# A hybrid attention encoder layer on one core: the first four loads on three queues, five spinning matmuls in place of six, and other queues for the last two stores

## The chip, the cores and the metric

The kernel runs on one core of one Trainium2 chip. The metric is device time of one execution in microseconds (us). Each kernel is run several times, and the median counts. One execution is also profiled: its span, and every instruction in it, is what the profile shows.

## The reference

One layer over x, 1024 tokens of 1024 channels in float32. A single projection `h = x @ W_in` gives queries, keys, values and gates of two groups of heads. Group A attends in a 2-D neighbourhood of the token grid with a learned bias, group B in a window of 128 with rotary positions and a sink. Each output is multiplied by SiLU of its gate, all are projected by `W_out`, and the layer ends in a layer norm:

```python
h = jnp.einsum('bsd,de->bse', x, w_in[layer])
q_a, k_a, v_a, z_a, q_b, k_b, v_b, z_b = jnp.split(h, SPLIT_POINTS, axis=-1)
...
mixed = jnp.concatenate([y_a * jax.nn.silu(z_a), y_b * jax.nn.silu(z_b)], axis=-1)
y = jnp.einsum('bse,ed->bsd', mixed, w_out[layer])
x = layer_norm(DEEPNORM_ALPHA * x + y, ln_gain[layer], ln_bias[layer])
```

## The kernel before

All matmuls of weights are made of three products: each operand is split into a high and a low part, and high by high, low by high and high by low are added up in PSUM.

**The head.** The first stage computes the values v of both groups, 640 columns, for tokens in tiles of 128. It walks over the eight slices k of 128 channels. For each k it needs one tile of x (`xT[half, k]`, 128 channels by 512 tokens) and one of the weights (`wv[k]`, 128 by 640). `load_x` and `load_wv` are generators that yield after every instruction, so that `interleave` can emit a load, a cast to the high part and a subtraction for the low part of both in turn. The rounding of wv to its high part runs on ScalarE (L414), that of x on VectorE for the first tile and on ScalarE for the others (L398), and the low parts on VectorE (L401, L417).

Only for k=0 are the tiles loaded in two pieces: `load_wv(0, (0, 320, 640))` and `load_x(0, 0, (0, 256, 512))`. Three calls of `next` ahead of the interleaving put the order of the four issues on the queue of SyncE (SP in the profile): left wv, left x, right x, and then right wv. The raw tiles come from pools of three buffers (wv) and four (x), so the loads for k=1 and k=2 go out at once behind these, and from k=3 on SyncE waits for a buffer.

The matmuls `v_mms` (L430) have x as their stationary operand and wv as the moving one, 320 columns at a time, in eight banks: four token tiles `t` by two halves `a` of wv. For k=0 the passes are the outer loop: first high by high over all eight banks, the left half of wv for the four token tiles and then the right half, then the two other passes. So the first two matmuls need the left wv and the left x, the third and fourth the right x, and the fifth to eighth the right wv. From k=1 on the three passes of one bank stand together, so that the second matmul of k=1 needs the low part of the second x tile.

Ahead of these, a memset of `warm` and six matmuls on it (L390) keep TensorE busy; nothing reads their result. GpSimd (POOL) builds the identity `identf` at the same time, which a transpose reads much later (L453). ScalarE's first instruction is the load of its activation table.

From the value stage on the order of instructions is written out by hand (`manual_schedule`); the part ahead of it is ordered by a scheduler.

**The tail.** After the last output matmuls of the eighth token tile, `norm_last` normalises its 1024 columns in three parts: `h0`, columns 0 to 255, and `h1`, 256 to 863, on VectorE (L968, L971 and then L975 for `h1` and `h0` in this order), and `h2`, the last 160, on ScalarE and GpSimd (L970, L972, L973). The stores of `h1` and `h0` are issued by SyncE (L976), that of `h2` by ScalarE (L977).

Of the kernel before, what the change touches and what calls it, by code (L numbers as in the profile page):

```python
# [55 lines left out]
def hybrid_block(ctx, tc, xT, x, wt, wv, wo, bias, sink, gain, lbias, cos, sin, bmask, out):  # L56
    nc = tc.nc
# [10 lines left out]
    def bank(tag):  # L68
        bufs = {"pj": 2, "s": 4, "t": 2}[tag]
        return (ps1 if bufs == 1 else ps2).tile([128, 512], F32, tag=tag, name=f"ps_{tag}", bufs=bufs)  # L70
# [311 lines left out]
    with ExitStack() as vctx:  # L382
# [3 lines left out]
        warm = vp.tile([128, 512], F16, name="warm", bufs=1)  # L386
        nc.vector.memset(warm, 0.0)
        ps = bank("t")
        for _ in range(6):
            nc.tensor.matmul(ps, warm[:, :128], warm, start=True, stop=True)  # L390

        def load_x(half, k, cuts=(0, 512)):
            raw = vp.tile([128, 512], F32, tag="xr", name="xraw", bufs=4)
            for a, b in zip(cuts, cuts[1:]):
                nc.sync.dma_start(raw[:, a:b], xT[half, k, :, a:b])
                yield
            for a, b in zip(cuts, cuts[1:]):
                (nc.scalar.copy if len(cuts) == 2 else nc.vector.tensor_copy)(xh[half, k][:, a:b], raw[:, a:b])  # L398
                yield
            for a, b in zip(cuts, cuts[1:]):  # L400
                nc.vector.tensor_sub(xl[half, k][:, a:b], raw[:, a:b], xh[half, k][:, a:b].bitcast(F32))  # L401
                yield

        def load_wv(k, cuts=(0, 640)):
            raw = vp.tile([128, 640], F32, tag="wvr", name="wvraw", bufs=3)
            for a, b in zip(cuts, cuts[1:]):
                nc.sync.dma_start(raw[:, a:b], wv[k, :, a:b])
                yield
            h = vw.tile([128, 640], F32R, name=f"wvh{k}")
            l = vw.tile([128, 640], F32R, name=f"wvl{k}")  # L410
            wvh.append(h)
            wvl.append(l)
            for a, b in zip(cuts, cuts[1:]):
                nc.scalar.copy(h[:, a:b], raw[:, a:b])  # L414
                yield
            for a, b in zip(cuts, cuts[1:]):
                nc.vector.tensor_sub(l[:, a:b], raw[:, a:b], h[:, a:b].bitcast(F32))  # L417
                yield
# [75 lines left out]
        banks = [bank(t) for t in tags]  # L494
        ordered.enter_context(tc.manual_schedule())
        first = load_wv(0, (0, 320, 640)), load_x(0, 0, (0, 256, 512))
        for i in (0, 1, 1):
            next(first[i])
        interleave(*first)
        interleave(load_wv(1), load_x(0, 1))  # L500
        for k in range(KT):
            if k + 2 < KT:
                interleave(load_wv(k + 2), load_x(0, k + 2))
            if k >= X1AT:
                interleave(load_x(1, 2 * (k - X1AT)))
                interleave(load_x(1, 2 * (k - X1AT) + 1))
                x_max(0, k - X1AT)
            for ps in ([0], [1], [2]) if k == 0 else ([0, 1, 2],):
                for a in range(2):
                    for t in range(4):  # L510
                        v_mms(banks[2 * t + a], t, a, k, ps)
# [240 lines left out]
    def quad(q):  # L752
        g, p, j, t, _ = units[4 * q]
        return g, p, j, t // 4 if g == "b" else t[0] // 2
# [161 lines left out]
    def final():  # L916
# [32 lines left out]
        def row_stats(t):  # L949
            mv = fp.tile([128, 2], F32, tag="mv", name="mv")  # L950
            nc.vector.bn_aggr(mv, stats[t][:, :4 if t == 7 else 2, :])  # L951
            sd = fp.tile([128, 1], F32, tag="sd", name="sd")
            nc.scalar.activation(sd, mv[:, 1:2], AF.Sqrt, bias=eps)  # L953
            return mv, sd

        def row_scale(mv, sd):
            rstd = fp.tile([128, 1], F32, tag="rstd", name="rstd")
            nc.vector.reciprocal(rstd, sd)
            nmr = fp.tile([128, 1], F32, tag="nmr", name="nmr")
            nc.vector.scalar_tensor_tensor(nmr, mv[:, 0:1], -1.0, rstd, op0=ALU.mult, op1=ALU.mult)  # L960
            return rstd, nmr

        def norm_last(t):
            ts = slice(128 * t, 128 * t + 128)
            xr = xrs[t]
            mv, sd = row_stats(t)
            h0, h1, h2 = slice(0, 256), slice(256, 864), slice(864, 1024)
            nc.vector.scalar_tensor_tensor(xr[:, h0], xr[:, h0], mv[:, 0:1], gb[:, h0], op0=ALU.subtract, op1=ALU.mult)  # L968
            rstd, nmr = row_scale(mv, sd)
            nc.scalar.activation(xr[:, h2], xr[:, h2], AF.Identity, bias=nmr, scale=rstd)  # L970
            nc.vector.scalar_tensor_tensor(xr[:, h1], xr[:, h1], mv[:, 0:1], gb[:, h1], op0=ALU.subtract, op1=ALU.mult)  # L971
            nc.gpsimd.tensor_mul(xr[:, h2], xr[:, h2], gb[:, h2])  # L972
            nc.gpsimd.tensor_add(xr[:, h2], xr[:, h2], bb[:, h2])  # L973
            for h in (h1, h0):
                nc.vector.scalar_tensor_tensor(xr[:, h], xr[:, h], rstd, bb[:, h], op0=ALU.mult, op1=ALU.add)  # L975
                nc.sync.dma_start(out[ts, h], xr[:, h])  # L976
            nc.scalar.dma_start(out[ts, h2], xr[:, h2])  # L977

        def norm(t):
            ts = slice(128 * t, 128 * t + 128)  # L980
# [44 lines left out]
        with tc.manual_schedule():  # L1025
            norm_last(7)
# [11 lines left out]
    for i in range(-LD, NU + LO):  # L1038
# [5 lines left out]
        per, h = divmod(i, 16)  # L1044
# [23 lines left out]
        q, m = divmod(i - LP - 3, 4)  # L1068
        if i >= Q30 + 2:
            q, m = (NU // 4 - 2, i - Q30 - 2) if i < Q30 + 4 else divmod(i - LP - 3, 4)  # L1070
        elif i >= Q30:
            q, m = -1, 0
# [9 lines left out]
        if 0 <= q < NU // 4:  # L1082
            g, p, j, h = quad(q)
# [88 lines left out]
```

## Time and profile before

| | |
|---|---|
| median of three runs | 455.44 us (455.09 to 457.77) |
| the profiled execution | 455.45 us |
| its span | 453.7 us |
| TensorE busy with matmuls | 443.1 us, 98% of the span |
| VectorE, ScalarE, GpSimd busy | 333.9, 288.0 and 228.1 us |
| DMA, mean over the span | 181 GB/s |

Times in the profile count from the start of the span. PE is TensorE's matmul row and PEld its row of weight loads, DVE is VectorE, ACT ScalarE, POOL GpSimd and SP SyncE; a q behind a name is the sequencer of that engine, which issues DMAs. The page cuts the span into 40 slices of 11.3 us:

```profile
PE   8999999999999999999999999999999999999993
...
DMA  7897278984557796687889779999989877004511
```

Each digit is a busy share in tenths. TensorE is short of nine tenths only in the first slice and the last, and these hold the lines that are changed.

### The profile page before, as it was taken

The page shows a single profiled execution, that of the slowest core. Times are in us where ns is not written, and L with a number is a line of the kernel's source. Part 1 is how long each engine was busy: PE and PEld are TensorE (multiplying, and loading weights), DVE is VectorE, ACT ScalarE, POOL GpSimd, SP SyncE. Part 2 cuts the span into 40 slices and gives each one's busy share as a digit, 9 for nine tenths or more (in the row PEclk, how much of TensorE's full clock was granted, in tenths as well). Part 3 has the DMA queues.
Part 4 walks back from the last instruction along what each step waited for, and adds up shares of the span by engine and source line. Part 5 has one row for each costly group of instructions (what it writes and reads, how often), then busy time and mean ns, then how long its engine had stood idle before and what let it go on. Part 6 is the DMA issues. An engine that isn't in the chain of part 4 may idle for free.

```text
span 453.7 us, 9395 instructions
## 1 busy us (share of the span) xinstructions
PE 443.1 (98%) x3239; PEld 293.1 (65%) x3239; DVE 333.9 (74%) x808; ACT 288.0 (63%) x664; POOL 228.1 (50%) x235
## 2 busy tenths in 40 slices
PE   8999999999999999999999999999999999999993
PEld 6999974444445565555555656555556788888883
DVE  5885956538987777896888878877878739099644
ACT  5648649776489877788778887686878824012100
POOL 0003944546948559688326766446663444007621
PEclk9999999999999999999999999999999999999997
DMA  7897278984557796687889779999989877004511
GB/s 249 291 320 266 76 247 259 309 307 177 208 103 167 151 176 152 112 176 139 167 154 174 174 161 216 190 175 232 188 166 225 165 230 286 0 17 147 187 54 61
DMA packets 134415, 82.28 MB, mean 181 GB/s; under 512 B 101344, under 2 KB 113504, under 8 KB 134112
## 3 DMA queue, kind: packets, MB, share of 16 engines
q1 hardware_dynamic: 134224, 81.61, 72.3%
q8 instruction: 25, 0.41, 0.4%
q14 instruction: 22, 0.18, 0.2%
q10 hardware_dynamic: 144, 0.08, 0.1%
HBM read 51.25 MB, written 9.96 MB: 135 GB/s over the span
## 4 chain that ended last, share of the span: by engine, by line
PE 91%; DVE 3%; issue 2%; ACT 2%; DMA 1%; SPq 0%; DVEq 0%; ACTq 0%
PE ps_pj L356 44%; PE ps_s L899 9%; PE ps_t L774 6%; PE ps_s L430 6%; PE ps_pj L899 6%; PE ps_t L899 5%; PE ps_s L709 4%; PE ps_s L710 4%; PE ps_pj L430 3%; PE ps_t L430 3%; PE ps_t L794 1%; DVE qs L241 1%; DMA wvraw<-in_wv 1%; ACT split L745 1%; DVE split L746 1%
## 5 line engine op out<-in xcount | busy, mean ns | idle before, releaser
L356 PE MATMUL ps_pj<-xf,wh 128*128 128x512 f16 x672 | 202.1, 379 | 0.9 <-DVE qs L241 0.6
L356 PE MATMUL ps_pj<-xf,wl 128*128 128x512 f16 x336 | 127.3, 379 | 0.0
L356 PEld LDWEIGHTS <-wh 128*128 128x128 f16 x672 | 63.5, 98 | 61.6 <-DVE ks L241 1.1
L735 ACT ACTIVATE ps_s<-sn,nm 128x385 f32<-128x385 f32 (+3 forms) x128 | 70.3, 549 | 32.8 <-DVE nm L719 31.7
L746 DVE SCALAR_TENSOR_TENSOR split<-ps_s,split 128x384 f16<-128x384 f32 (+2 forms) x128 | 65.7, 513 | 27.7 <-ACT split L745 26.3
L745 ACT ACTIVATE split<-ps_s 128x384 f16<-128x384 f32 (+2 forms) x128 | 57.6, 450 | 1.8
L356 PEld LDWEIGHTS <-wl 128*128 128x128 f16 x336 | 32.9, 98 | 37.4
L719 DVE CUSTOM_DVE_ANT_0 sn<-ps_s,bm,nsk 128x384 f32<-128x384 f32 (+1 forms) x64 | 40.8, 638 | 6.8 <-PE ps_s L710 6.2
L899 PE MATMUL ps_s<-wo,m 128*128 128x512 f32 (+1 forms) x192 | 43.3, 379 | 0.0
L719 DVE CUSTOM_DVE_ANT_0 sn<-ps_s,bias,sg 128x264 f32<-128x264 f32 (+1 forms) x64 | 35.0, 548 | 10.9 <-PE ps_s L710 4.7
L187 POOL TENSOR_SCALAR wr<-wr,wsc 128x512 f32<-128x512 f32 x26 | 20.7, 796 | 39.8 <-ACT wh L182 33.7
L709 PE MATMUL ps_s<-ks,qs 128*128 128x384 f16 (+4 forms) x128 | 39.3, 307 | 0.0
L710 PE MATMUL ps_s<-ks,qs 128*128 128x384 f16 (+4 forms) x128 | 39.2, 306 | 0.0
L899 PEld LDWEIGHTS ps_s<-wo,m 128*128 128x128 f32 x192 | 34.4, 188 | 7.0
L774 PEld LDWEIGHTS <-tr 128*128 128x128 f16 (+1 forms) x1104 | 36.5, 98 | 2.2 <-issue 0.3
L681 POOL TENSOR_SCALAR bias<-bias,rsg 128x552 f32<-128x552 f32 (+1 forms) x24 | 19.3, 802 | 36.4 <-DMA bias<-in_bias 25.5
L953 ACT ACTIVATE sd<-mv,eps 128x1 f32<-128x1 f32 x8 | 2.4, 295 | 50.5 <-DVE mv L951 46.5
L188 POOL TENSOR_TENSOR wl<-wr,wh 128x512 f16<-128x512 f32 x26 | 32.6, 1256 | 2.2
L273 POOL COPY ks<-ks 64x512 f16<-64x512 f16 x40 | 26.4, 666 | 10.9 <-DVE ks L241 6.1
L989 POOL TENSOR_TENSOR xr<-xr,gb 128x512 f32<-128x512 f32 x7 | 10.3, 1474 | 40.8 <-ACT xr L986 40.8
L430 PE MATMUL ps_s<-wvh,x 128*128 128x320 f32 x128 | 29.5, 310 | 0.0
L899 PE MATMUL ps_pj<-wo,m 128*128 128x512 f32 (+1 forms) x120 | 28.7, 377 | 0.0
(147 smaller groups left out, 825.6 us busy)
## 6 DMA issues: line engine op xcount, KB each, us to landing
xraw<-in_xT SPq DMA_DIRECT2D x31, 256.0 KB, 4.3
ws<-in_wt SPq DMA_DIRECT2D x15, 512.0 KB, 5.2
wr<-in_wt SPq DMA_DIRECT2D x26, 256.0 KB, 3.0
bias<-in_bias SPq DMA_DIRECT2D x16, 276.0 KB, 3.4
wor<-in_wo SPq DMA_DIRECT2D x16, 256.0 KB, 3.2
xr<-in_x SPq DMA_DIRECT2D x8, 512.0 KB, 7.3
out<-xr SPq DMA_DIRECT2D x14, 256.0 KB, 2.1
bias<-in_bias SPq DMA_DIRECT2D x8, 368.0 KB, 3.9
```

Source lines behind the costliest of these rows:

```text
L188: nc.gpsimd.tensor_sub(l, raw, h)
L273: nc.gpsimd.tensor_copy(t[o, sl], t[a, sl])
L356: nc.tensor.matmul(ps, a[:, k % 4, :], mv, start=(k == 0 and i == 0), stop=(k == KT - 1 and i == 2))
L430: nc.tensor.matmul(ps[:, :320], lh[t // 4, k][:, ts], rh[k][:, cs], start=(k == 0 and i == 0), stop=(k == KT - 1 and i == 2))
L709: nc.tensor.matmul(ps[:, :m], q, sl[0], start=True, stop=False)
L710: nc.tensor.matmul(ps[:, :m], q, sl[1], start=False, stop=True)
L719: nc.vector.tensor_tensor_reduce(sn[:, :m], ps[:, :m], bias_t, sg[:, c:c + 1], init, op0=ALU.add, op1=ALU.min, accum_out=nm)
L735: nc.scalar.activation(pt[:, :m], sn[:, :m], AF.Exp, bias=nm, scale=-1.0, accum_out=sm[:, k:k + 1])
L745: nc.scalar.activation(hl[:, :m, 0, :c], src, AF.Copy, scale=PSCALE)
L746: nc.vector.scalar_tensor_tensor(hl[:, :m, 1, :c], src, PSCALE, hl[:, :m, 0, :c], op0=ALU.mult, op1=ALU.subtract)
L774: nc.tensor.matmul(ps[:, HD * m:HD * m + HD], a, b_, start=(i == 0), stop=(i == len(mms) - 1))
L899: nc.tensor.matmul(ps, lh[:, ts], rh[:, cs], start=(e == EO[0] and i == 0), stop=(e == EO[-1] and i == 2))
```

## The change

The four first loads are spread over three queues. `load_x` with three cuts (the first tile alone) issues its left piece from ScalarE and its right piece from SyncE; `load_wv` issues the left or only piece from SyncE and, where there is a second, that one from GpSimd. The spinning matmuls are five. In `norm_last` the store of `h0` goes to ScalarE and that of `h2` to SyncE, behind that of `h1`.

```diff
-        for _ in range(6):
+        for _ in range(5):
             nc.tensor.matmul(ps, warm[:, :128], warm, start=True, stop=True)
...
-            for a, b in zip(cuts, cuts[1:]):
-                nc.sync.dma_start(raw[:, a:b], xT[half, k, :, a:b])
+            for q, a, b in zip((nc.scalar, nc.sync) if len(cuts) == 3 else (nc.sync,), cuts, cuts[1:]):
+                q.dma_start(raw[:, a:b], xT[half, k, :, a:b])
                 yield
...
-            for a, b in zip(cuts, cuts[1:]):
-                nc.sync.dma_start(raw[:, a:b], wv[k, :, a:b])
+            for q, a, b in zip((nc.sync, nc.gpsimd), cuts, cuts[1:]):
+                q.dma_start(raw[:, a:b], wv[k, :, a:b])
                 yield
...
-            for h in (h1, h0):
+            for h, q in ((h1, nc.sync), (h0, nc.scalar)):
                 nc.vector.scalar_tensor_tensor(xr[:, h], xr[:, h], rstd, bb[:, h], op0=ALU.mult, op1=ALU.add)
-                nc.sync.dma_start(out[ts, h], xr[:, h])
-            nc.scalar.dma_start(out[ts, h2], xr[:, h2])
+                q.dma_start(out[ts, h], xr[:, h])
+            nc.sync.dma_start(out[ts, h2], xr[:, h2])
```

In the order of instructions on each engine nothing else moves. ScalarE's new load stands ahead of its table load. GpSimd's stands between the memset of `identf` and the instruction that makes the identity of it. On SyncE the order behind is left wv, right x, wv for k=1, x for k=1, and so on as before.

## The prediction

> **What bounds the kernel now.** I read the page first: TensorE (PE) is busy 443.1 us of a 453.7 us span, so only about 10.6 us are open at all. The table of waits, asked for TensorE alone, has four entries: 1.3 us until the spinning matmuls start, 0.7 us in the first projection step, and 0.6 and 0.4 us in the middle. The change touches the first ten microseconds and the last four. So the chain of waits of the first 14 us comes next (start, length, what):
>
> ```profile
> 0.74 0.39 SPq L407
> 1.19 0.42 SPq L395
> 1.65 0.43 SPq L395
> 2.12 3.02 DMA wvraw<-in_wv
> 5.17 0.47 ACT wvh L414
> 5.68 0.41 PE ps_pj L430
> ```
>
> SyncE issues the four first loads one after the other, some 0.46 us apart. The fourth, the right half of the first wv tile, takes 3.02 us to land, ScalarE rounds it, and TensorE then goes on. The timeline shows both sides of that wait and the next place where loads and TensorE meet (start, length, engine, line, operation, idle time before it):
>
> ```profile
> 1.33 2.74 PE L390 MATMUL ps_t<-warm 128*128 128x512 f16 x6 [1.33 <-DVE warm L387]
> 3.92 0.60 PE L430 MATMUL ps_pj<-wvh,x 128*128 128x320 f32 x1
> ...
> 4.70 0.30 PE L430 MATMUL ps_s<-wvh,x 128*128 128x320 f32 x1
> ...
> 5.68 0.41 PE L430 MATMUL ps_pj<-wvh,x 128*128 128x320 f32 x1 [0.67 <-ACT wvh L414]
> ...
> 7.40 0.62 ACT L398 CAST x<-xraw 128x512 fp32r<-128x512 f32 x1 [0.34 <-DMA xraw<-in_xT]
> ...
> 8.05 0.69 DVE L401 TENSOR_TENSOR x<-xraw,x 128x512 fp32r<-128x512 f32 x1
> ...
> 8.72 0.49 PE L430 MATMUL ps_pj<-wvh,x 128*128 128x320 f32 x2
> ```
>
> From 5.68 the matmuls start 0.147 us apart. The fourth started at 4.70, so the fifth could have started at 4.85: the wait is worth 5.68 - 4.85 = 0.83 us. But look at step k=1: its second matmul needs the low part of the second x tile, ready at 8.05 + 0.69 = 8.74, and TensorE is there at 8.72 + 0.15 = 8.87. The slack is 0.1 us. Whatever is gained in step k=0 waits again in k=1, unless that x tile lands earlier too. So the landing of the second x tile (7.40 now) is the row that prices the change. Step k=2 doesn't matter: its x cast ends at 9.50 and TensorE needs it near 12.1.
>
> Is that landing limited by issue or by the DMA engines? The windows of a quarter microsecond answer (window, length, busy time of each engine, clock, DMA share, GB/s):
>
> ```profile
> 4.00:4.25 0.25, 0.25 (x2) 0.25 (x2) 0.25 (x2) 0.00 (x0) 0.00 (x0) 1.00 1.21 297
> 4.75:5.00 0.25, 0.25 (x2) 0.00 (x0) 0.25 (x2) 0.00 (x0) 0.00 (x0) 1.00 0.70 261
> 5.00:5.25 0.25, 0.00 (x1) 0.00 (x0) 0.22 (x1) 0.08 (x1) 0.00 (x0) 1.00 0.59 205
> 5.25:5.50 0.25, 0.00 (x0) 0.00 (x0) 0.00 (x0) 0.25 (x1) 0.00 (x0) 1.00 0.58 219
> 6.00:6.25 0.25, 0.25 (x4) 0.25 (x3) 0.15 (x1) 0.00 (x0) 0.00 (x0) 1.00 1.00 383
> ```
>
> The sixteen engines are nearly full except between 4.75 and 5.50, a hole of 0.25 x (0.30 + 0.41 + 0.42) = 0.28 us, and in the ramp from 1.75 to 2.50 (shares 0.59, 0.82 and 0.92, so 0.17 us). The tail, timeline again:
>
> ```profile
> 448.83 1.72 DVE L975 SCALAR_TENSOR_TENSOR xr<-xr,rstd,bb 128x608 f32<-128x608 f32 x2
> 449.31 0.95 POOL L973 TENSOR_TENSOR xr<-xr,bb 128x160 f32<-128x160 f32 x1
> 449.91 0.99 SPq L976 DMA_DIRECT2D out<-xr  x2
> 450.29 0.37 ACTq L977 DMA_DIRECT2D out<-xr  x1
> ```
>
> SyncE's two issues take 0.33 each in 0.99 us, so the second starts at 450.57, just after VectorE's last result at 450.55: it waits for its data and not for the queue. The last two parts already leave on two queues.
>
> **The change part by part.** *Loads.* The left half of x goes from SyncE's second place (1.19) to ScalarE's first instruction (0.73). The one ScalarE DMA that the trace has was issued in 0.37 us, as fast as SyncE's. The activation table load (1.28 us from 0.73) moves behind it and ends near 2.45; ScalarE's first cast waits for data until 2.96, so 0.5 us of that cover is left and the cost is nothing. The right half of x moves on SyncE from 1.65 to 1.19. The right half of wv leaves SyncE (2.12) for GpSimd, behind one memset that ends at 0.93. The mask instruction for the identity behind it is delayed, and its first reader is the transpose at 38.1: nothing. Everything behind on SyncE (second wv tile, second x tile and so on) is issued two places earlier: 2 x 0.46 = 0.92 us.
>
> The first matmul (3.92) needs the left wv (landed 2.96, cast 0.46) and the left x (landed 3.48, cast 0.29). Both transfers now start together and share the engines. By the bytes both should be there when both were before, near 3.48: then the wv cast ends at 3.94 where x was ready at 3.77, so the start moves by 0.0 to 0.3 us later. The wait of 0.83 absorbs that: the fifth matmul waits for the right wv, issued up to 1.2 us earlier, and 576 KB in all must land, which before was at 5.17.
>
> So the gain is how much earlier the second x tile lands. Bounds: 0 if the engines' share alone counts; 0.92 if issue alone counts, of which TensorE can use the 0.83. Between them I take 0.3: the hole of 0.28 is what a slow load at the head of a single queue leaves, and it is the part that three queues can fill; of the ramp I count almost nothing.
>
> *Five spinning matmuls.* 2.74 us for six, their weight loads 0.43 apart: the sixth frees TensorE near 3.86, the fifth near 3.43. The first real weight load was at 3.89, with x ready at 3.77: at most 0.1 us, and none where data come at 3.9 or later. Zero.
>
> *Tail.* The last 256 columns go to ScalarE, the 160 columns to SyncE, free at 450.24 when its data are done at 450.26. Issue to landing is 2.1 us on SyncE and 2.2 on ScalarE in the table of DMA issues. Bounds -0.05 (an own queue) and +0.1; I take +0.05.
>
> Sum against the profiled execution: 455.45 (span 453.7 and 1.75 around it), which is also the median of the runs (455.44): 455.45 - 0.3 + 0.05 = 455.2. TensorE waits only 1.0 us after the head and before the tail, so the shift passes through.
>
> **The rivals.** *The transfers only interleave.* The windows speak for it: shares near 1 before and after the hole, and 1152 KB must land before k=1 can go on. Then the 0.83 moves from k=0 to the second matmul of k=1, the gain is 0, and with the tail the time is 455.5. The Trainium skill says this outright (DMA: Bandwidth & Descriptors, "Issuing engines are not separate DMA queues"): loads from several engines run on the same sixteen DMA engines, and only the issue time is saved. By that rule this rival holds; the trace agrees in the full windows and not in the hole.
>
> *GpSimd's load comes late: slower.* No load in this trace is issued by GpSimd. The place is the fifth matmul, and it decides from a landing at 5.1 on; from there a microsecond costs a microsecond. The nearest rows, 160 KB on SyncE, took 2.2 and 3.0 us: from 0.93 that is 3.1 to 3.9, well before. The longest of the head (the third x tile, 4.8) gives 5.7, a loss of 0.6 and 456.1; with another microsecond for a first use, 457.1. Against it stands 1.2 us of margin. The Trainium skill (SBUF — State Buffer, "SBUF: two separate sides") warns that descriptors written by GpSimd wait while VectorE holds the port they share. Here VectorE does two short memsets until 1.27 and then nothing until 3.48, so the trace gives it little to hold.
>
> *The clock comes later: slower too.* The spinning matmuls run 0.43 us per 512 columns, the real ones from 5.68 on 0.147 per 320: 0.83 against 0.46 ns a column, though the granted clock reads 1.00 throughout. The switch came near 4.5, after 3.2 us of work from 1.33. With five spins TensorE idles from 3.46 to about 3.9. If the count began anew at the first real matmul (3.9), TensorE would run slowly to 7.1, which is 12 of the 24 matmuls of k=0, and do the other 12 in 1.8 us, to 8.9 where it now ends near 8.72; begun anew behind the wait, near 5.0, it would run slowly to 8.2, 16 matmuls in all, and end at 9.4. A loss of 0.2 to 0.7: 455.9. Against it: the gap of 0.83 before 5.68 did not slow anything.
>
> *The whole wait is collected.* If the second x tile lands by 6.6, nothing waits and all of 0.83 is gained: 454.7.
>
> **How the numbers follow.** Forecast 455.2 (its own range 454.9 to 455.4): 0.45. Interleaving, 455.5: 0.20. GpSimd late, 456.1: 0.15. Clock late, 455.9: 0.10. All collected, 454.7: 0.10. The range 454.5 to 456.5 leaves out the far end of the two slow cases. About 1% (4.55 us) is what a measurement of this kernel can tell from no change; its three runs alone span 2.7 us. No case comes near 450.9 or 460.0. I leave 0.02 and 0.03 for what I don't see.
>
> **What would show it.** Right: the idle time before the fifth projection matmul shrinks from 0.67 to under 0.2, the cast of the second x tile starts near 7.1, step k=1 waits a little before its second matmul, and the tail from VectorE's last result to the end of the span is as long as before (3.1 us). Interleaving: that cast at 7.4 still. GpSimd late: ScalarE's second cast after 5.2, released by GpSimd's load. Clock: projection matmuls 0.27 us apart after 5 us. The forecast is wrong in its mechanism if the second x tile lands earlier by 0.3 and the span is not shorter, or if the time moves by over 1 us.

## The result and the profile after

The changed kernel takes 457.95 us (median of 22 runs), the kernel before on the same chip 455.99 us (22 runs). The ratio is 1.0031, with a 95% interval from 1.0016 to 1.0046: slower by 0.3%. The two medians are further apart (1.96 us), because that of the changed kernel falls into the upper of two groups of runs; the means of all runs are 1.41 us apart, as the ratio has it. Counts and ranges of runs below leave out one disturbed run of 574 us, of the kernel with eight spins.

The runs of the changed kernel fall into two groups. Eight lie between 455.93 and 456.78, fourteen between 457.50 and 459.46. Of the kernel before, four of 22 lie above 457. The profiled execution (span 457.0, 3.3 us longer than before) is one of the upper group.

The chain of waits of its first 14 us, with start, length and what:

```profile
1.30 4.97 DMA wvraw<-in_wv
...
6.29 0.47 ACT wvh L414
...
6.80 0.63 PE ps_pj L430
7.43 0.27 PE ps_s L430
...
11.17 0.27 PE ps_s L430
11.44 0.25 PE ps_pj L430
11.69 0.14 PE ps_s L430
```

The load of the right half of the first wv tile, now GpSimd's, is still the link that everything waits for. It took 3.02 us from issue to landing, and takes 4.97 now. Behind it the matmuls of step k=0 stand 0.27 us apart up to 11.5 us, where before they stood 0.15 apart from the fifth on. The timeline gives the same stretch instruction by instruction:

```profile
1.30 0.74 POOL L407 DMA_DIRECT2D wvraw<-in_wv  x1 [0.35 <-issue]
...
1.34 2.31 PE L390 MATMUL ps_t<-warm 128*128 128x512 f16 x5 [1.34 <-DVE warm L387]
...
3.44 0.46 ACT L414 CAST wvh<-wvraw 128x320 fp32r<-128x320 f32 x1 [0.97 <-DMA wvraw<-in_wv]
...
4.07 0.61 PE L430 MATMUL ps_pj<-wvh,x 128*128 128x320 f32 x1 [0.41 <-DVE x L398]
...
6.80 0.63 PE L430 MATMUL ps_pj<-wvh,x 128*128 128x320 f32 x1 [1.33 <-ACT wvh L414]
...
7.65 0.62 ACT L398 CAST x<-xraw 128x512 fp32r<-128x512 f32 x1
...
11.96 0.46 PE L430 MATMUL ps_pj<-wvh,x 128*128 128x320 f32 x2
```

The fifth real matmul starts at 6.80, 1.12 us later than before. Step k=1 starts at 11.96 where it started at 8.72: from the fifth matmul to there it takes 5.16 us, where it took 3.04. So 2.12 us more are the slow matmuls, 1.12 the wait: 3.24 in all. Idle time stands now ahead of the first real matmul too (0.41), where the sixth spin stood. And the second x tile, issued 0.94 us earlier, is cast from 7.65 on, not from 7.40: nothing was won there.

The four loads, from the table of DMA issues for the first 1.9 us (size, and us from issue to landing):

```profile
wvraw<-in_wv SPq DMA_DIRECT2D x1, 160.0 KB, 2.7
wvraw<-in_wv POOLq DMA_DIRECT2D x1, 160.0 KB, 5.0
xraw<-in_xT ACTq DMA_DIRECT2D x1, 128.0 KB, 2.9
xraw<-in_xT SPq DMA_DIRECT2D x1, 128.0 KB, 2.7
```

Before, these took 2.2, 3.0, 2.3 and 2.2. The prediction had seen a hole in the DMA share between 4.75 and 5.50 us (0.70, 0.59 and 0.58). Three quarter-microsecond windows of the changed kernel show where it went (the last two numbers are the DMA share and GB/s):

```profile
2.00:2.25 0.25, 0.25 (x2) 0.08 (x1) 0.00 (x0) 0.25 (x1) 0.15 (x2) 1.00 0.23 36
...
3.75:4.00 0.25, 0.00 (x0) 0.00 (x0) 0.24 (x2) 0.14 (x1) 0.00 (x0) 1.00 0.57 102
...
5.25:5.50 0.25, 0.22 (x1) 0.00 (x0) 0.04 (x1) 0.00 (x0) 0.00 (x0) 1.00 1.03 305
```

From 4.75 to 5.50 the shares are now 1.03, 0.69 and 1.03, but from 2.00 to 2.50 they are 0.23 and 0.57 and from 3.50 to 4.25 they are 0.55, 0.57 and 0.43. Over 1.50 to 5.50 the engines moved 212 GB/s, before 228. The hole was filled and others opened earlier. The tail, timeline:

```profile
451.88 1.71 DVE L975 SCALAR_TENSOR_TENSOR xr<-xr,rstd,bb 128x608 f32<-128x608 f32 x2
452.37 0.95 POOL L973 TENSOR_TENSOR xr<-xr,bb 128x160 f32<-128x160 f32 x1
452.96 0.33 SPq L976 DMA_DIRECT2D out<-xr  x1
453.39 0.38 SPq L977 DMA_DIRECT2D out<-xr  x1
453.63 0.36 ACTq L976 DMA_DIRECT2D out<-xr  x1
```

From VectorE's last result (453.59) to the end of the span are 3.39 us, before 3.11. Sum against the profile of before: 3.24 in the head, 0.28 in the tail and 0.2 less in the 437 us between them make the 3.3.

### The profile page after: what moved, and what is told of

Read it like the earlier page. It is cut to its first block, busy times and chain, and to the rows that moved or that the text cites. A ratio compares the mean times of both kernels' runs of the same rounds, so it can differ in the third digit from the quotient of the medians.

```text
span 457.0 us, 9394 instructions
## 1 busy us (share of the span) xinstructions
PE 445.1 (97%) x3238; PEld 295.3 (65%) x3238; DVE 333.6 (73%) x808; ACT 287.8 (63%) x664; POOL 228.4 (50%) x236
## 4 chain that ended last, share of the span: by engine, by line
PE 91%; DVE 3%; issue 2%; ACT 2%; DMA 1%; DVEq 0%; POOL 0%; POOLq 0%; ACTq 0%
PE ps_pj L356 44%; PE ps_s L899 9%; PE ps_t L774 6%; PE ps_s L430 6%; PE ps_pj L899 6%; PE ps_t L899 5%; PE ps_s L709 4%; PE ps_s L710 4%; PE ps_pj L430 3%; PE ps_t L430 3%; PE ps_t L794 1%; DMA wvraw<-in_wv 1%; DVE qs L241 1%; ACT split L745 1%; DVE split L746 1%
## 5 line engine op out<-in xcount | busy, mean ns | idle before, releaser
L430 PE MATMUL ps_s<-wvh,x 128*128 128x320 f32 x128 | 30.8, 320 | 0.0
```

The costliest lines, as they stand in the source:

```text
L430: nc.tensor.matmul(ps[:, :320], lh[t // 4, k][:, ts], rh[k][:, cs], start=(k == 0 and i == 0), stop=(k == KT - 1 and i == 2))
```

## The experiments

Twelve runs in four sets, each set beside the kernel before on the same chip. Theories A and B are about what makes the clock late: A the missing spin, B the long wait for the load. Theory C came after the first four.

**Five spins alone.** In the kernel before:

```diff
-        for _ in range(6):
+        for _ in range(5):
```

> The kernel before with five spinning matmuls; loads and stores as before. Theory A (the missing spin lets TensorE idle near 3.6 us, and the clock comes late): matmuls 0.27 us apart beyond 6 us in most runs, median about 457.3. Theory B (the long wait for GpSimd's load makes the clock late): the spin alone does nothing, median about 456.0 as before.

Measured: 456.23 against 455.64, ratio 1.0012 (1.0003 to 1.0022). In its profile the matmuls are 0.27 apart up to 6.8 us. One run of twelve lies above 457. The missing spin costs something, so B alone falls; it costs far less than the change, so A alone falls too.

**Six spins with the new loads and stores.** In the changed kernel:

```diff
-        for _ in range(5):
+        for _ in range(6):
```

> The changed kernel with six spinning matmuls. Theory A: the clock comes as early as before, and only the late load remains: median 456.5 to 457. Theory B: the fifth matmul still waits to 6.8 us and the clock is late: 458, as the changed kernel. Either way GpSimd's load lands near 6.3 us.

Measured: 456.46 against 455.64, ratio 1.0024 (1.0015 to 1.0033). In its profile the load lands at 5.6, a little better than expected, but matmuls stay slow to 10.0 us. That profile is of one of the two slowest runs (457.73); eight of the eleven runs lie between 456.18 and 456.61, and what the clock did in them is not shown. So the sixth spin does not bring the clock back in every run. The median is A's, the late clock of the profile B's.

**No GpSimd.** In the changed kernel the right wv is issued by ScalarE:

```diff
-            for q, a, b in zip((nc.sync, nc.gpsimd), cuts, cuts[1:]):
+            for q, a, b in zip((nc.sync, nc.scalar), cuts, cuts[1:]):
```

> The changed kernel with the right half of the first wv tile issued by ScalarE behind the left x, not by GpSimd; five spins. If the load was late because GpSimd issued it: it lands near 4.7 us, the fifth matmul starts near 5.3, and step k=1 waits for the second x tile near 7.4. If it was late because three queues share the engines: near 6 us again. Theory A: the clock is still late in most runs, median about 457; theory B: 455.7.

Measured: 456.79 against 455.64, ratio 1.0024 (1.0014 to 1.0034). The timeline of its profile:

```profile
4.07 0.90 ACT L414 CAST wvh<-wvraw 128x320 fp32r<-128x320 f32 x2 [1.15 <-DMA wvraw<-in_wv]
...
4.58 0.64 PE L430 MATMUL ps_pj<-wvh,x 128*128 128x320 f32 x1 [0.94 <-ACT wvh L414]
```

The right wv is there at 4.5, as expected without GpSimd, but the left one, which the first matmul needs, lands 1.1 us later than before (cast at 4.07, not 2.96). The idle time moved from the fifth matmul to the first. The clock rises at 9.3.

**Spins in the wait.** In the changed kernel, ahead of the fifth real matmul:

```diff
+                    if k == 0 and ps == [0] and a == 1:
+                        for _ in range(3):
+                            nc.tensor.matmul(banks[1], warm[:, :128], warm, start=True, stop=True)
                     for t in range(4):
```

> The changed kernel with three more spinning matmuls between the fourth and the fifth real one, into a bank that the fifth overwrites. The load stays late. If idle time of TensorE delays the clock, it comes before 8.2 us and the median is 456.5 to 457; if the clock has nothing to do with the idle time, 458 as the changed kernel.

Measured: 457.15 against 455.64, ratio 1.0030 (1.0017 to 1.0043), half of eight runs above 457. The profile, of a run in the faster half (456.38), did what was expected: the clock is up by 6.8, step k=1 starts at 9.59, the span is 454.6. The median did not, and from one profile it can't be said where the other runs lost their time. A miss.

These four profiles and those of the two kernels led to theory C. Until some moment, which is called here the rise of the clock, TensorE's matmuls of 320 columns start 0.27 us apart, and 0.15 us from there on. The Trainium skill (TensorE: Matmul & The Clock Gate, "Part 1: The HAM clock gate (the "warmup" mystery)") says that the clock is decided over windows of about 3.4 us that run on freely and don't start with the kernel. It does not say how much idle time such a window may hold. The table is an estimate, worked out from the starts of the matmuls with that page's figure for the window. Idle is all time beyond 0.43 us for a spinning matmul and 0.27 us for a slow real one, so it includes the slower start of a matmul behind a wait:

```
kernel               clock rises near   idle in the 3.4 us ahead   idle in the 3.4 us before those
before               4.6                0.4                        -
e1 five spins        6.8                0.7                        1.3
e4 spins in wait     6.1 to 6.8         0.8 to 0.9                 1.4 to 2.0
e2 loads, six spins  10.0               0.0                        1.35
e3 two queues        9.3                0.0                        1.3
changed kernel       11.5               0.0                        1.7, and 0.83 before that
```

Windows with up to 0.7 us of idle time raised the clock, those with 1.3 and more did not. Between them lies the border: the changed kernel's 0.83 did not raise it, and the fourth experiment's 0.8 to 0.9, by where in its stretch the rise is put, did. That the place of the windows is a matter of chance in each run is the page's statement; the two groups of runs agree with it, and the two profiles with eight spins, at the end of this section, show the rise at two places in one kernel.

**Ten spins.** In the changed kernel, so that nothing is idle until the load lands:

```diff
-        for _ in range(5):
+        for _ in range(10):
```

> The changed kernel with ten spinning matmuls, which reach to about 5.6 us, so that TensorE is not idle between 1.33 and the fifth real matmul. Theory C (the clock rises at the end of a stretch of some 3.4 us whose place differs from run to run, if TensorE idled less than about a fifth of it): it rises by 7.5 us in every run, the late load alone remains, median 456.3 to 456.8 and all runs within 1 us. Rival (the spread loads are slow by themselves, whatever the clock does): 457 to 458 and two groups of runs as before.

Measured: 456.50 against 455.94, ratio 1.0010 (1.0000 to 1.0020); eleven of twelve runs between 455.98 and 456.93, one at 457.59, so that the expected 1 us for all runs was missed by this one. Timeline:

```profile
1.34 4.45 PE L390 MATMUL ps_t<-warm 128*128 128x512 f16 x10 [1.34 <-DVE warm L387]
...
6.65 0.47 PE L430 MATMUL ps_pj<-wvh,x 128*128 128x320 f32 x1
6.92 0.42 PE L430 MATMUL ps_s<-wvh,x 128*128 128x320 f32 x1
...
7.17 0.31 PE L430 MATMUL ps_t<-wvh,x 128*128 128x320 f32 x1
```

Matmul lengths fall from 0.47 to 0.31 at 7.1, and the upper group is all but gone, although the loads are those of the changed kernel. C said this, the rival did not.

**Three spins.** In the kernel before, to make the clock late with its own loads:

```diff
-        for _ in range(6):
+        for _ in range(3):
```

> The kernel before with three spinning matmuls; loads and stores untouched. Theory C: TensorE idles 1.3 us from 2.6 to 3.9 and 0.8 us before the fifth real matmul, the clock rises between 7.3 and 10.7 us, and the median is 1.0 to 1.5 us above the kernel before. Rival: with the loads untouched nothing happens, below 0.3 us.

Measured: 456.97 against 455.94, ratio 1.0020 (1.0005 to 1.0034); six runs up to 456.51 and six from 457.44 on, the two groups of the changed kernel; of the kernel before beside them, six of 29 lie above 457. Timeline, of the slowest of the runs:

```profile
1.33 1.46 PE L390 MATMUL ps_t<-warm 128*128 128x512 f16 x3 [1.33 <-DVE warm L387]
3.95 0.60 PE L430 MATMUL ps_pj<-wvh,x 128*128 128x320 f32 x1 [1.16 <-DVE x L398]
...
6.16 0.64 PE L430 MATMUL ps_pj<-wvh,x 128*128 128x320 f32 x1 [0.81 <-ACT wvh L414]
...
11.66 0.53 PE L430 MATMUL ps_pj<-wvh,x 128*128 128x320 f32 x2
```

With 1.16 and 0.81 us idle the clock rises near 11.9. Idle time alone, without any change to a load, gives the picture of the changed kernel. (C's place for the rise, 7.3 to 10.7, was too early by one us: the right wv came at 5.65, half a us later than in the profile it was worked out from.)

**Only the left x on ScalarE.** In the kernel before:

```diff
-                nc.sync.dma_start(raw[:, a:b], xT[half, k, :, a:b])
+                q.dma_start(raw[:, a:b], xT[half, k, :, a:b])
```

with `q` ScalarE for the first of the two pieces.

> The kernel before with one edit: the left half of the first x tile is issued by ScalarE; six spins. If the issue on SyncE holds the head up: the right wv lands 0.4 us earlier, the second x tile 0.3 earlier, median 0.2 to 0.3 us below the kernel before. If the transfers only interleave: the left wv lands near 3.4 and not 2.95, the second x tile as before, median within 0.2 us.

Measured: 457.08 against 455.94, ratio 1.0014 (1.0000 to 1.0029), half of twelve runs above 457.4. The left wv lands later (its cast starts at 3.71, not 2.96), the second x tile is no earlier (7.74). The transfers interleave, as expected of the second theory, but that the time stays within 0.2 us was wrong. A later first matmul (4.22, not 3.92) is idle time for the clock, and that would explain it; but the profile is of a run in the lower group (455.90) with the clock up by 4.9, so this is argued here and not shown.

**Only the right wv on GpSimd.** In the kernel before:

```diff
-            for a, b in zip(cuts, cuts[1:]):
-                nc.sync.dma_start(raw[:, a:b], wv[k, :, a:b])
+            for q, a, b in zip((nc.sync, nc.gpsimd), cuts, cuts[1:]):
+                q.dma_start(raw[:, a:b], wv[k, :, a:b])
```

> The kernel before with one edit: the right half of the first wv tile is issued by GpSimd; six spins. If GpSimd's path is slow by itself: it lands at 5.6 to 6.3 as in the changed kernel, and the median is 0.5 to 0.9 us above the kernel before. If it was late because three queues shared the engines: it lands near 5.1 or earlier and the median is within 0.2 us.

Measured: 457.78 against 455.94 in six runs, ratio 1.0046 (1.0030 to 1.0063): by the ratio the slowest of all. From its DMA table and its timeline:

```profile
xraw<-in_xT SPq DMA_DIRECT2D x2, 128.0 KB, 2.8
wvraw<-in_wv SPq DMA_DIRECT2D x1, 160.0 KB, 2.3
wvraw<-in_wv POOLq DMA_DIRECT2D x1, 160.0 KB, 3.4
```

```profile
5.01 0.29 DVE L398 CAST x<-xraw 128x256 fp32r<-128x256 f32 x1 [1.22 <-DMA xraw<-in_xT]
```

GpSimd's load took 3.4 us and landed at 4.7. In the seven profiles with the loads of before, SyncE's lands between 4.5 and 5.6. So issuing it from GpSimd does not alone make it late, though its first packet starts 1.6 us after the issue, where SyncE's first load needs 1.0. But the right x, which SyncE issued after it, was cast at 5.01, in those seven profiles between 3.85 and 4.71, and the third matmul waited for it; the clock rose at 9.0. Both branches of the expectation fall: the load was early and the time was worse.

**A version that keeps TensorE busy.** In the kernel before, loads and stores untouched, with eight spins, then seven, then six and two more ahead of the fifth real matmul (the edit of the fourth experiment with 2 for 3):

```diff
-        for _ in range(6):
+        for _ in range(8):
```

> The kernel before with eight spinning matmuls; loads and stores untouched. Theory C: TensorE works from 1.33 to about 5.8 us without a pause, the clock rises by 7.5 us in every run, no run is above the kernel before's fast group by more than 1 us, and the median is 0 to 0.4 us below the kernel before. Rival (two more spins only push the real matmuls back): 0.3 to 0.8 us slower.

> The kernel before with seven spinning matmuls, which end near 4.3 us. Theory C: as with eight, with at most 0.7 us of idle time ahead of the fifth real matmul; median 0 to 0.3 us below the kernel before. Rival: 0.2 to 0.4 us slower.

> The kernel before with two more spinning matmuls between the fourth and the fifth real one, into a bank that the fifth overwrites; loads and stores untouched. Theory C: the wait for the right wv is filled, the clock rises by 7.5 us, median 0 to 0.4 us below the kernel before. Rival: where the right wv lands early they stand in its way, and the median is 0.2 to 0.5 us above.

Measured, against 455.65: 455.42 with eight, ratio 0.9990 (0.9978 to 1.0001), all runs between 455.10 and 455.77; 455.60 with seven, 0.9995 (0.9982 to 1.0008), none above 456.60; 455.79 with two in the wait, 1.0000 (0.9992 to 1.0009), none above 456.29, but not below the kernel before, as C had it. The kernel before reached 457.85 beside them. The timeline with eight:

```profile
1.33 3.28 PE L390 MATMUL ps_t<-warm 128*128 128x512 f16 x8 [1.33 <-DVE warm L387]
4.26 0.50 PE L430 MATMUL ps_pj<-wvh,x 128*128 128x320 f32 x1
4.59 0.30 PE L430 MATMUL ps_s<-wvh,x 128*128 128x320 f32 x1
```

Eight spins take 3.28 us and not 8 x 0.43, since the clock rises in the last of them. Then eight again:

> The kernel before with eight spinning matmuls a second time, since the first interval reached just to 1. Theory C: no run above 456.5 again, median 0.1 to 0.5 us below the kernel before, ratio 0.999. If the first result was chance: ratio 1.000, and some runs above 457.

Measured: 455.66 against 455.64, ratio 0.9996 (0.9988 to 1.0005); all runs between 454.88 and 455.88, while the kernel before reached 456.93. So more spins take away the late runs, as C says: none of 23 runs with eight lies above 456, and of the kernel before, beside them, 8 of 45 do. But the median is not shown to be better than before; C's 0.1 us or more did not come again. Against the changed kernel the gain is clear. The timeline of this second profile:

```profile
1.33 3.59 PE L390 MATMUL ps_t<-warm 128*128 128x512 f16 x8 [1.33 <-DVE warm L387]
...
5.25 0.47 PE L430 MATMUL ps_t<-wvh,x 128*128 128x320 f32 x1
5.52 0.37 PE L430 MATMUL ps_s<-wvh,x 128*128 128x320 f32 x1
```

It is the kernel of the first profile, on another chip, and here too TensorE works without a pause from 1.33 on; but the clock rises near 5.5, where in the first it rose near 4.2. With ten spins under the new loads, also without a pause, it rose at 7.1. So it took 2.9, 4.2 and 5.8 us of unbroken work: the rise does not come after a fixed amount of work.

The fourteen profiles of this case, put in order of the rise (the first real matmul of at most 0.37 us), are in order of time too, nearly one by one. Six rise by 5.6 us and took 454.96 to 455.90; three between 6.8 and 7.2 took 456.26 to 456.59; two near 9 took 456.93 and 457.00; three at 10.0 and later took 457.73 to 458.75. Kernels with the old loads and with the new ones stand in this one order. And by the estimate of the table, the eight profiles that came after it keep to its border: the stretches that raised the clock held up to 0.6 us of idle time, those just before them 0.96 or more.

## Why the prediction was wrong

The forecast was 455.2, by 0.3 us faster; the result is slower by 0.3%, some 1.4 us by the ratio. By its steps:

- **"The landing of the second x tile is the row that prices the change" and "I take 0.3".** The sum's main term came out at nothing. The tile was issued 0.94 us earlier and landed no earlier: its cast starts at 7.65, 6.90, 7.49, 7.15 and 6.87 in the five profiles with left x and right wv both moved (mean 7.21), and at 7.40, 6.81, 7.59, 7.13, 6.56, 7.64 and 7.23 in the seven with the loads of before (mean 7.19). The first rival, that the transfers only interleave, was right on this point, and so was the rule of the Trainium skill that the prediction set beside it (DMA: Bandwidth & Descriptors, "Issuing engines are not separate DMA queues"). The hole in the DMA share between 4.75 and 5.50 was taken for room that more queues would fill and so gain time. They filled it, but left as much room open earlier (0.23 and 0.57 from 2.00 to 2.50).
- **"The first matmul moves by 0.0 to 0.3 us later. The wait of 0.83 absorbs that."** It moved by 0.15 in the profile. The wait absorbed it as TensorE's time, but it is idle time, and idle time was not free: it went into the clock.
- **"GpSimd's load comes late", with 1.2 us of margin.** This rival occurred, with the sign that was named for it (ScalarE's second cast after 5.2): landing at 6.27, so a loss of 1.1 where 0.6 was priced. Its far row, 4.8 us to land, was the right one (4.97). GpSimd did add to it: it started 0.35 us after its memset, issued for 0.74 us, where SyncE needs 0.4, and its first packet started 1.6 to 2.3 us after the start of the issue in the five profiles that have this load, where SyncE alone needs 1.0. But with only this load moved it landed at 4.7. With left x on ScalarE as well, and three loads issued before it, it landed between 5.4 and 6.3 in four profiles. That sharing is the reason is argued, not shown.
- **"The clock comes later", chance 0.10, price 0.2 to 0.7.** This is the step that failed most: the sum put the clock at nothing. The mechanism was named, with the sign that came (matmuls 0.27 us apart after 5 us), and the argument against it, that the gap of 0.83 before 5.68 did not slow anything, was drawn from a profile where the clock had risen ahead of that gap. The price counted slow matmuls to 7.1 or 8.2; they went on to 11.5, which cost 2.1 us. It was worked out from a switch after 3.2 us of work, which one profile had shown; in three other profiles it took 2.9, 4.2 and 5.8 us of work without a pause. Fourteen of 22 runs lie in the upper group. Keeping TensorE busy under the same loads brings the ratio from 1.0031 to 1.0010, so by the middles of the two intervals, which were taken on different chips and overlap a little, about two thirds of the loss, 1.0 us of 1.4, is the clock; the profile's 2.1 us of 3.3 is the same share.
- **"Five spinning matmuls: zero."** Wrong: alone 1.0012 (0.6 us). In its profile the first real matmul started no later (3.84), but the clock rose at 6.8: a spin is worth more than the time that it blocks.
- **The tail, +0.05.** The reasoning held: the second store did wait for its data, and nothing was gained. The size was off. From VectorE's last result to the end of the span are 3.11 to 3.14 us in the profiles with neither edit, 3.24 with the stores moved and no load on GpSimd, 3.28 with that load and the old stores, and 3.37 to 3.39 with both. So the stores cost 0.1 us, the upper bound of the prediction, and the one load on GpSimd 0.15 at the far end of the kernel, a term that the sum did not have.
- **The 0.95 left for a time within 1%.** That held, but no rival had been given a loss as large as this one, except at the far end of GpSimd's (457.1).

What stays open: why spreading the first loads delays the one that is needed first by more than its share (left wv's cast at 4.07 with two queues), how much of GpSimd's late landing is its own path and how much the sharing, and what lengthened the runs with spins in the wait.

## What to carry to other kernels

At the start of a kernel, idle time of TensorE costs twice: once as a wait, and once more if it holds back the clock, at up to 2 us here. Judge spinning matmuls by whether they bridge to the data without a pause, and take off none before the data are shown to come earlier; and when the DMA engines are nearly full, as here, spreading loads over queues can change which one is late without landing the last any sooner, so keep the order in which they are needed.

## What the runs showed of the hardware that was not expected

Two queues that start together moved less in their first half microsecond than one. The windows of 2.0 to 2.5 us, of the kernel before and then of the changed kernel (the last two numbers are the DMA share and GB/s):

```profile
2.00:2.50 0.50, 0.50 (x2) 0.15 (x1) 0.00 (x0) 0.01 (x1) 0.00 (x0) 1.00 0.87 275
```

```profile
2.00:2.50 0.50, 0.50 (x2) 0.15 (x1) 0.00 (x0) 0.47 (x1) 0.34 (x2) 1.00 0.40 105
```

275 GB/s fell to 105, and the first transfer landed 0.5 us later (2.7 us after its issue, not 2.2). All fourteen profiles agree. In the six where ScalarE issues the left x beside SyncE's left wv, this window has 68 to 140 GB/s and the left wv lands after 2.7 to 3.3 us; in the eight others 238 to 286 GB/s and 2.2 to 2.4 us. In the six, the first packet of one of the two queues starts at 1.77 to 1.78 us, as with one queue, and that of the other at 1.90 to 2.42. Why is open. The granted clock reads 1.00 in every window, also where matmuls run at half the rate: it doesn't show the rise that decided this case. The spacing of the matmuls does. By an estimate from it, a microsecond at 0.27 us a matmul in place of 0.147 costs about 0.45 us; from the profile with the earliest rise (4.3 us, 454.96) to that with the latest (11.9 us, 458.33) this makes 3.4 us, and the runs are 3.4 us apart, though they differ in their waits for loads too.
